# The last level of block inverses in three visits: two pairs of heads one step apart

## The chip, the core and the metric

The kernel runs on one core of a Trainium2 chip. The metric is the time of one execution on the device in microseconds; before the change the median of three runs is 1191.49 (1191.37 to 1192.41).

## The reference, cut to what matters

One layer of a decoder trunk, for 1024 tokens of width 1024 in float32. After an RMSNorm one projection feeds two mixers: four heads of a gated delta rule (head size 128, chunks of 64 in the reference) and eight heads of dilated window attention. Their outputs go through an output projection, a residual, a gated MLP with a causal convolution, and a last norm. The change touches the delta rule, which solves a unit lower triangular system for each chunk and head:

```python
lmat = dec_strict * kk * bc[..., None, :]
rhs = jnp.concatenate([vc, gam * kc], axis=-1)
sol = lax.linalg.triangular_solve(lmat, rhs, left_side=True, lower=True, unit_diagonal=True)
...
def step(state, xs):
    u = uv - jnp.einsum('bhck,bhkv->bhcv', wk, state)
    o = jnp.einsum('bhck,bhkv->bhcv', qd, state) + jnp.einsum('bhcj,bhjv->bhcv', at, u)
    state = ge[..., None, None] * state + jnp.einsum('bhck,bhcv->bhkv', ke, u)
```

## The kernel before

The kernel works with chunks of 128 tokens, so each of the four heads has eight (`NCH`) 128x128 triangles to invert. VectorE inverts the 32x32 blocks on the diagonal (`forward_sub`, line 684). `merges` (line 712) then joins them on TensorE: first 32x32 blocks to 64x64, then, in the part that is changed, 64x64 blocks to 128x128. The transposed result lies in `y` (the tile named um in the profile), one tile for each head; `x64` holds the 64x64 inverses, one tile for a pair of heads (`e` is 0 or 1 within the pair). In that last level every head and chunk needs two products in a row:

- the first ("down") contracts over partitions 0 to 63 (`lo`) and writes a bank's partitions 64 to 127 (`up`), `w2ps`; a copy brings it to `x64[up, e]` (ScalarE for `e` = 0, VectorE for `e` = 1);
- the second ("up") contracts over partitions 64 to 127 and writes partitions 0 to 63, `y2ps`; it reads what the first copy left, and a second copy brings it with its sign turned to `y[lo, :, up]`.

Before, one visit makes the 32 down products of all four heads, a second visit the 32 up products. In the profile a down product is ps<-x,um and an up product ps<-um,x, both 64*64 64x64; each float32 product leaves two matmul records, a product of fp32r operands one. The banks have the tags `asc` and `ch`, two banks each.

The order of instructions on TensorE comes from a planner, the class `Weave` (line 46). Each part of the program is a generator; it yields the time until its operands are ready by the planner's own costs (`need`, line 95, with a slack: `MSLACK` is 1.5 us), and meanwhile the planner runs another part. `mm` (line 191) hands it the cost of a product as its last number, and stamps the products in the order in which they are made. The filler in this stretch is the dense input projection, `dense` (line 508): columns of 128 outputs, each in two halves (`hh`) of eight groups; a group is three products (`mm3`, line 204: xhi,whi, xlo,whi, xhi,wlo, each 128x512). When a half column ends, VectorE scales it out of its bank (`scaled`, line 444, aqkv in the profile); behind the second half come the next weights' split, whi on ScalarE and wlo on VectorE (`split`, line 210), and for some columns a transpose on VectorE (avt).

When all four heads are merged, `chain` (line 811) runs the recurrence over the eight chunks, four heads in turn, with 128x128 products: r,um (the solve), wke,ktok (the new state), ct,kT and ct,qat (with the state ct) and w,qat. Its first products are ps<-vtok,um. The small operations between them (r, wke, ct, vtok) are VectorE's, w is ScalarE's. Attention follows (`attention`, line 915): scores, softmax in tiles sm (a reduction, an exponential on ScalarE, a reciprocal and a multiply on VectorE, two of each a pair of blocks), half transposes of the probabilities (`tp_half`, line 199, ps<-ident,sm) and value products (pt,vn and pb,vc). Then come the output projection and the MLP.

Of the kernel before, what the change touches and what calls it, by code (L numbers as in the profile page):

```python
# [9 lines left out]
AF = mybir.ActivationFunctionType  # L10
OP = mybir.AluOpType
# [7 lines left out]
H = 4  # L19
NCH = 8  # L20
# [16 lines left out]
MSLACK = 1.5  # L37
# [107 lines left out]
def hybrid_layer(tc, I, out):  # L145
    nc = tc.nc
    wv = Weave()
    ve = Engine(wv, nc.vector, "vector", 0.07, 0.00105)
    ac = Engine(wv, nc.scalar, "scalar", 0.12, 0.00085)
# [16 lines left out]
    def tile_(pool, shape, dt, name, tag, bufs):  # L166
        return wv.slot(pool.tile(list(shape), dt, name=name, tag=tag, bufs=bufs), tag, bufs)
# [3 lines left out]
    def A(name, tag, dt=F32, shape=(P, 1024)):  # L171
        if tag in TURNS:
            i = turns[tag] = turns.get(tag, -1) + 1
            tag = TURNS[tag][i % len(TURNS[tag])]
        return tile_(lp, shape, dt, name, tag, SLOTS[tag])
# [12 lines left out]
    def after(inst, anchor, reason="keeps a slot free until it is needed"):  # L188
        tc.add_manual_dep(inst.ins, anchor.ins.name, order, reason=reason)

    def mm(dst, lhs, rhs, us, start=True, stop=True, **kw):
        tc.stamp_issue_order_token(nc.tensor.matmul(dst, lhs, rhs, start=start, stop=stop, **kw).ins, TOKEN)  # L192
        wv.product(us, dst, lhs, rhs)
# [64 lines left out]
    def bank(tag, name="ps"):  # L258
        return tile_(pp_, (P, 512), F32, name, tag, 2)
# [237 lines left out]
    G = [dict() for _ in range(H)]  # L497
# [186 lines left out]
    def forward_sub():  # L684

        mt_t = A("mt", "go")
        sy.dma_start(mt_t, mdram.rearrange("h p f -> (h p) f"))
        mt = mt_t.rearrange("p (j i) -> p j i", j=32)
        xi_t = A("xi", "go")
        xi = xi_t.rearrange("p (i c) -> p i c", i=32)  # L690
        tmp = tile_(sp, [P, 256], F32, "tmp", "t1", 1)
        po_.memset(xi, 0.0)
        po_.affine_select(xi, xi, pattern=[[1, 32], [-1, 32]], compare_op=OP.not_equal, fill=1.0, base=0,
                                channel_multiplier=0)

        free = wv.free["vector"]
        for j in range(31):
            ni, ncol = 31 - j, j + 1
            tv = tmp[:, :ni * ncol].rearrange("p (i c) -> p i c", i=ni)
            ve.tensor_tensor(tv, mt[:, j, j + 1:, None].to_broadcast([P, ni, ncol]),  # L700
                                    xi[:, j, None, :ncol].to_broadcast([P, ni, ncol]), op=OP.mult)
            ve.tensor_tensor(xi[:, j + 1:, :ncol], xi[:, j + 1:, :ncol], tv, op=OP.subtract)

        ve.tensor_copy(mt, xi.rearrange("p i c -> p c i"))
        sy.dma_start(xtdram.rearrange("h p f -> (h p) f"), mt_t)
        anchor = sy.dma_start(xdram.rearrange("h p f -> (h p) f"), xi_t)
        wv.free["vector"] = free
        wv.add(2, merges(anchor))
# [3 lines left out]
    def merges(anchor):  # L712

        tags = ("asc", "ch")
        yield wv.need(xdram)
        ys = [G[h].pop("um") for h in range(H)]
        x64s = []
        for pair in range(2):
            x64 = A("x64", "go", shape=(P, 2, NCH, 64))
            x64s.append(x64)  # L720
            after(po_.memset(x64, 0.0), anchor)
            xd = xdram[2 * pair:2 * pair + 2].rearrange("h (c r) (i j) -> r i (h c) j", r=4, i=32)
            for r in range(4):
                b, o = slice(32 * r, 32 * r + 32), 32 * (r % 2)
                sy.dma_start(x64[b, :, :, o:o + 32].rearrange("p h c j -> p (h c) j"), xd[r])
            for h in (2 * pair, 2 * pair + 1):
                xtd = xtdram[h].rearrange("(c r) (j i) -> r j c i", r=4, j=32)
                for r in range(4):
                    b = slice(32 * r, 32 * r + 32)
                    sy.dma_start(ys[h][b, :, b], xtd[r])  # L730

        heads = [(h, ys[h], x64s[h // 2], h % 2) for h in range(H)]
        halves = [(slice(64 * p, 64 * p + 32), slice(64 * p + 32, 64 * p + 64)) for p in range(2)]

        def four(t):
            return t.rearrange("p (h c j) -> p h c j", h=2, c=NCH)

        w1ps = [bank(t) for t in tags]
        yield wv.need(*w1ps, *x64s, *ys, slack=4.5)
        for h, y, x64, e in heads:  # L740
            for c in range(NCH):
                for a, b in halves:
                    mm(four(w1ps[h // 2])[b, e, c, :], y[a, c, b], x64[a, e, c, 0:32], 0.02)
        w1s = []
        for p in w1ps:
            w1 = tile_(sp, [P, 2, NCH, 32], F32, "w1", "t2", 2)
            w1s.append(w1)
            ac.activation(w1[halves[0][1]], four(p)[halves[0][1]], AF.Copy)
            ve.tensor_copy(w1[halves[1][1]], four(p)[halves[1][1]])
        y1ps = [bank(t) for t in tags]  # L750
        yield wv.need(*y1ps, *w1s, slack=MSLACK)
        for h, y, x64, e in heads:
            w1, y1v = w1s[h // 2], four(y1ps[h // 2])
            for c in range(NCH):
                for a, b in halves:
                    mm(y1v[a, e, c, :], w1[b, e, c, :], y[b, c, b], 0.01)
                b = halves[0][1]
                mm(y1v[b, e, c, :], y[b, c, b], w1[b, e, c, :], 0.02)
        for pair in range(2):
            x64, y1v = x64s[pair], four(y1ps[pair])  # L760
            ve.tensor_scalar(x64[32:64, :, :, 0:32], y1v[32:64], -1.0, None, op0=OP.mult)
            if pair == 1:
                po_.tensor_copy(mark[32:33], x64[32:33, 0, 0, 0:1])
            for i, (a, b) in enumerate(halves):
                for e in range(2):
                    y = ys[2 * pair + e]
                    if (i, e) == (1, 1):
                        ve.tensor_scalar(y[a, :, b], y1v[a, e], -1.0, None, op0=OP.mult)
                    else:
                        ac.activation(y[a, :, b], y1v[a, e], AF.Copy, scale=-1.0)  # L770

        lo, up = slice(0, 64), slice(64, 128)
        w2ps = [bank(t) for t in tags for _ in range(2)]
        yield wv.need(*w2ps, *x64s, *ys, slack=MSLACK)
        w2vs = [p.rearrange("p (c j) -> p c j", c=NCH) for p in w2ps]
        for h, y, x64, e in heads:
            for c in range(NCH):
                mm(w2vs[h][up, c, :], y[lo, c, up], x64[lo, e, c, :], 0.067)
        for h, y, x64, e in heads:
            if e == 0:  # L780
                last["merged"] = ac.activation(x64[up, e], w2vs[h][up], AF.Copy)
            else:
                ve.tensor_copy(x64[up, e], w2vs[h][up])
        wv.done.add("merged")
        y2ps = [bank(t) for t in tags for _ in range(2)]
        yield wv.need(*y2ps, *x64s, slack=MSLACK)
        for h, y, x64, e in heads:
            y2v = y2ps[h].rearrange("p (c j) -> p c j", c=NCH)
            for c in range(NCH):
                mm(y2v[lo, c, :], x64[up, e, c, :], y[up, c, up], 0.067)  # L790
        for h, y, x64, e in heads:
            y2v = y2ps[h].rearrange("p (c j) -> p c j", c=NCH)
            if e == 0:
                ac.activation(y[lo, :, up], y2v[lo], AF.Copy, scale=-1.0)
            else:
                ve.tensor_scalar(y[lo, :, up], y2v[lo], -1.0, None, op0=OP.mult)
            G[h]["yt"] = y
            wv.done.add(("m", h))

    def chain_load(h, s):  # L800
# [285 lines left out]
    last = {}  # L1086
# [696 lines left out]
```

## Time and profile before

| | |
|---|---|
| median of three runs | 1191.49 us |
| profiled execution, time | 1191.63 us |
| its span in the profile | 1189.8 us |
| TensorE busy | 1180.1 us, 99% |
| VectorE busy | 965.4 us, 81% |
| ScalarE busy | 573.2 us, 48% |
| granted TensorE clock, mean | 0.998 |

The page and the answers of the trace name TensorE's matmuls PE, its weight loads PEld, VectorE DVE, ScalarE ACT, GpSimd POOL and the queue that issues most transfers SP. Matmuls are pipelined, so a record is longer than the distance to the next; costs on PE are read from starts. A line of a timeline gives start and length in microseconds, the operation with output<-inputs, its tile sizes and a count of merged records, and in brackets idle time of the engine before it and what ended that.

### The profile page before, as it was taken

The numbers are of one execution on the slowest core, as the hardware profiler recorded it, in microseconds if no ns is written. First come the engines' busy times: TensorE is split into PE (matmuls) and PEld (weight loads), VectorE is DVE, ScalarE is ACT, GpSimd is POOL, SyncE is SP. The second block draws the span as 40 slices with busy tenths as digits, with TensorE's granted clock in tenths as the row PEclk, the third lists the DMA queues.
The fourth block names the chain that finished last, engine by engine and source line by source line (L and its number), as shares of the span: only waits on it lengthen the run. The fifth ranks groups of instructions, "written<-read, shape, count | busy, mean of one in ns | idle before, by whom it ended". The sixth has DMA issues, their size and how long they took to land.

```text
span 1189.8 us, 18253 instructions
## 1 busy us (share of the span) xinstructions
PE 1180.1 (99%) x6994; PEld 975.9 (82%) x6994; DVE 965.4 (81%) x1545; ACT 573.2 (48%) x1122; POOL 54.6 (5%) x49
## 2 busy tenths in 40 slices
PE   9999999999999999999999999999999999999997
PEld 7888888888777777888888888888888888888887
DVE  7776996474677787677998898989889889898987
ACT  7473444363434444555554444545444553546452
POOL 0212001013000000000000000000000000000001
PEclk9999999999999999999999999999999999999999
DMA  7423457647552414343221313122231395356734
GB/s 239 107 94 84 114 144 163 201 149 186 166 147 72 99 37 151 142 159 107 89 92 68 107 53 107 57 103 81 80 102 58 120 377 202 124 178 220 239 98 160
DMA packets 114520, 156.91 MB, mean 132 GB/s; under 512 B 54368, under 2 KB 65408, under 8 KB 114432
## 3 DMA queue, kind: packets, MB, share of 16 engines
q1 hardware_dynamic: 113712, 155.21, 41.4%
q8 instruction: 55, 0.90, 0.3%
q10 hardware_dynamic: 720, 0.53, 0.1%
q14 instruction: 33, 0.27, 0.1%
HBM read 117.68 MB, written 38.03 MB: 131 GB/s over the span
## 4 chain that ended last, share of the span: by engine, by line
PE 97%; DVE 1%; ACT 0%; issue 0%; DVEq 0%; ACTq 0%
PE ps L192 47%; PE pa L192 20%; PE dw L192 18%; PE pc L192 10%; PE ps L201 1%; PE ps L196 1%; PE warm L192 0%; DVE x1h L139 0%; ACT sm L141 0%; DVE sm L141 0%; PE pd L192 0%; DVE avt L139 0%; DVE aqkv L139 0%; DVE wke L141 0%; DVE ct L141 0%
## 5 line engine op out<-in xcount | busy, mean ns | idle before, releaser
L192 PE MATMUL dw<-pr 128*128 128x512 f32 (+1 forms) x984 | 211.4, 376 | 0.0
L192 PEld LDWEIGHTS dw<-pr 128*128 128x128 f32 x984 | 176.7, 188 | 33.7
L192 PE MATMUL ps<-xhi,whi 128*128 128x512 f32 x448 | 183.7, 410 | 0.0
L192 PE MATMUL ps<-xhi,wlo 128*128 128x512 f32 x448 | 175.2, 391 | 0.0
L192 PE MATMUL ps<-xlo,whi 128*128 128x512 f32 x448 | 174.9, 391 | 0.0
L192 PE MATMUL pa<-T,pair 128*128 128x512 f32 x528 | 126.8, 389 | 0.0
L192 PEld LDWEIGHTS pa<-T,pair 128*128 128x128 f32 x528 | 99.1, 188 | 20.6
L192 PEld LDWEIGHTS ps<-xhi,whi 128*128 128x128 f32 x448 | 84.2, 188 | 18.9 <-issue 2.7
L192 PEld LDWEIGHTS ps<-xhi,wlo 128*128 128x128 f32 x448 | 84.1, 188 | 18.3
L192 PEld LDWEIGHTS ps<-xlo,whi 128*128 128x128 f32 x448 | 84.4, 188 | 14.9 <-DVE xlo L139 0.3
L139 ACT ACTIVATE u<-pa 128x512 f32<-128x512 f32 x44 | 26.4, 599 | 114.4 <-PE pa L192 114.4
L139 DVE SCALAR_TENSOR_TENSOR y<-xu,fcw,y 128x1023 f32<-128x1023 f32 (+1 forms) x44 | 56.4, 1281 | 22.1 <-ACT y L139 22.0
L139 ACT ACTIVATE pr<-wd 128x1024 fp32r<-128x1024 f32 x33 | 35.0, 1061 | 73.4 <-DVE wd L139 35.8
L192 PE MATMUL pa<-B,A 128*128 128x512 f32 x264 | 63.5, 389 | 0.0
L192 PE MATMUL pc<-B,pair 128*128 128x512 f32 x264 | 63.4, 389 | 0.0
L192 PE MATMUL pc<-T,S 128*128 128x512 f32 x264 | 63.4, 389 | 0.0
L192 PE MATMUL pa<-T,S 128*128 128x512 f32 x264 | 63.4, 389 | 0.0
L139 DVE TENSOR_TENSOR wst<-wst 128x512 f32<-128x512 f32 x88 | 60.4, 686 | 0.8
L139 ACT ACTIVATE whi<-wst 128x1024 fp32r<-128x1024 f32 (+2 forms) x38 | 38.5, 1013 | 46.5 <-PE ps L192 38.9
L192 PE MATMUL ps<-B,pair 128*128 128x512 f32 x252 | 60.5, 389 | 0.0
L141 ACT ACTIVATE sm<-sm,mx 128x128 f32<-128x128 f32 (+7 forms) x64 | 35.5, 556 | 49.7 <-DVE mx L141 49.7
L192 PEld LDWEIGHTS pa<-T,S 128*128 128x128 f32 x264 | 49.6, 188 | 10.3
(248 smaller groups left out, 2229.8 us busy)
## 6 DMA issues: line engine op xcount, KB each, us to landing
wst<-in_wu SPq DMA_DIRECT2D x44, 512.0 KB, 3.7
wd<-in_wd SPq DMA_DIRECT2D x44, 512.0 KB, 4.4
wst<-in_wi SPq DMA_DIRECT2D x25, 512.0 KB, 4.2
upark<-y SPq DMA_DIRECT2D x22, 512.0 KB, 3.6
r<-upark SPq DMA_DIRECT2D x22, 512.0 KB, 9.9
wa<-in_wd SPq DMA_DIRECT2D x22, 256.0 KB, 3.0
apark<-aqkv SPq DMA_DIRECT2D x8, 512.0 KB, 2.7
wst<-in_wo SPq DMA_DIRECT2D x8, 512.0 KB, 3.6
```

The lines of the kernel that those rows point to most:

```text
L139: return getattr(eng, op)(*a, **kw)
L141: return getattr(eng, op)(*a, **kw)
L192: tc.stamp_issue_order_token(nc.tensor.matmul(dst, lhs, rhs, start=start, stop=stop, **kw).ins, TOKEN)
L196: tc.stamp_issue_order_token(nc.tensor.transpose(dst, src, ident).ins, TOKEN)
L201: tc.stamp_issue_order_token(nc.tensor.transpose(dst, src[rows], ident[rows, rows]).ins, TOKEN)
```

## The change

The last level takes three visits in place of two. The first makes the down products of heads 0 and 1; the second makes the up products of heads 0 and 1 and the down products of heads 2 and 3 in turn, one of each; the third makes the up products of heads 2 and 3. The copies keep their engines. Each visit takes its own banks, and the costs that the planner is told change from 0.067 to 0.06 for a product that stands alone and 0.035 for one in turn. The mark `merged`, for which the values of head 3 wait, is set behind the second visit.

```diff
-        w2ps = [bank(t) for t in tags for _ in range(2)]
-        yield wv.need(*w2ps, *x64s, *ys, slack=MSLACK)
-        w2vs = [p.rearrange("p (c j) -> p c j", c=NCH) for p in w2ps]
-        for h, y, x64, e in heads:
-            for c in range(NCH):
-                mm(w2vs[h][up, c, :], y[lo, c, up], x64[lo, e, c, :], 0.067)
-        for h, y, x64, e in heads:
-            if e == 0:
-                last["merged"] = ac.activation(x64[up, e], w2vs[h][up], AF.Copy)
-            else:
-                ve.tensor_copy(x64[up, e], w2vs[h][up])
-        wv.done.add("merged")
-        y2ps = [bank(t) for t in tags for _ in range(2)]
-        yield wv.need(*y2ps, *x64s, slack=MSLACK)
-        for h, y, x64, e in heads:
-            y2v = y2ps[h].rearrange("p (c j) -> p c j", c=NCH)
-            for c in range(NCH):
-                mm(y2v[lo, c, :], x64[up, e, c, :], y[up, c, up], 0.067)
...
+        w2ps, y2ps = {}, {}
+        for step in range(3):
+            downs = heads[2 * step:2 * step + 2]
+            ups = heads[2 * step - 2:2 * step] if step else []
+            w2ps.update({h: bank(tags[step]) for h, *_ in downs})
+            y2ps.update({h: bank(tags[step % 2 - 1]) for h, *_ in ups})
+            yield wv.need(*[w2ps[h] for h, *_ in downs], *[y2ps[h] for h, *_ in ups], *x64s, *ys, slack=MSLACK)
+            for i in range(2):
+                for c in range(NCH):
+                    for h, y, x64, e in ups[i:i + 1]:
+                        mm(cols(y2ps[h])[lo, c, :], x64[up, e, c, :], y[up, c, up], 0.06 if not downs else 0.035)
+                    for h, y, x64, e in downs[i:i + 1]:
+                        mm(cols(w2ps[h])[up, c, :], y[lo, c, up], x64[lo, e, c, :], 0.06 if not ups else 0.035)
+            for h, y, x64, e in downs:
+                if e == 0:
+                    last["merged"] = ac.activation(x64[up, e], cols(w2ps[h])[up], AF.Copy)
+                else:
+                    ve.tensor_copy(x64[up, e], cols(w2ps[h])[up])
...
+            if step == 1:
+                wv.done.add("merged")
```

The copies of the up products and the marks `("m", h)` that release the chain are as before, at the end of each step and behind the loop.

More of the change, by code (lines that the diff above doesn't have):

```diff
@@ L784, in merges, with cols @@
-        wv.done.add("merged")
-        y2ps = [bank(t) for t in tags for _ in range(2)]
-        yield wv.need(*y2ps, *x64s, slack=MSLACK)
-        for h, y, x64, e in heads:
-            y2v = y2ps[h].rearrange("p (c j) -> p c j", c=NCH)
-            for c in range(NCH):
-                mm(y2v[lo, c, :], x64[up, e, c, :], y[up, c, up], 0.067)
[L791 to L797, printed above, removed]
+        def cols(p):
+            return p.rearrange("p (c j) -> p c j", c=NCH)
@@ new lines, in merges @@
+        w2ps, y2ps = {}, {}
[16 more added lines that the diff above has]
+                    ve.tensor_copy(x64[up, e], cols(w2ps[h])[up])
+            for h, y, x64, e in ups:
+                if e == 0:
+                    ac.activation(y[lo, :, up], cols(y2ps[h])[lo], AF.Copy, scale=-1.0)
+                else:
+                    ve.tensor_scalar(y[lo, :, up], cols(y2ps[h])[lo], -1.0, None, op0=OP.mult)
+                G[h]["yt"] = y
+            if step == 1:
+                wv.done.add("merged")
@@ L798, in merges @@
+        for h in range(H):
             wv.done.add(("m", h))
```

## The prediction

> **What bounds the kernel now.** I read the profile's page first, then who TensorE (PE) waited for, then the busy time by stage, and at the end the timelines of PE and VectorE (DVE) around the changed level and in the stages behind it.
>
> ```profile
> PE 1180.1 (99%) x6994; PEld 975.9 (82%) x6994; DVE 965.4 (81%) x1545; ACT 573.2 (48%) x1122; POOL 54.6 (5%) x49
> PE 97%; DVE 1%; ACT 0%; issue 0%; DVEq 0%; ACTq 0%
> ```
> ```profile
> PE warm L192 <- DVE pick L139: 1.1, 1, 1.1
> PE ps L196 <- DVE rs L139: 0.7, 1, 0.7
> PE ps L192 <- ACT w L141: 0.5, 1, 0.5
> PE ps L192 <- DVE ct L141: 0.4, 1, 0.4
> PE ps L192 <- ACT sq L139: 0.3, 1, 0.3
> PE ps L201 <- DVE sm L141: 0.3, 1, 0.3
> ```
> ```profile
> 560.00:900.00 340.00, 340.00 (x1506) 281.59 (x1505) 302.63 (x345) 164.77 (x217) 0.22 (x1) 1.00 0.25 82
> ```
>
> The first row is the page's busy time, the second its chain that ended last, the six are all of PE's waits (total, times, longest), the last a stage of the MLP. PE carries 97% of the chain, and its waits sum to 3.3 us of 1189.8. In the MLP PE has no gap (340.00 of 340.00 us) with DVE at 302.63. So a microsecond of PE time saved at 210 us comes off the end, unless DVE takes it back before 450 us; behind that each engine's order of instructions is the same in both programs. The change is therefore priced by PE's spacing in its own stretch, and by what DVE does to PE in the two stages after it.
>
> **The two old visits.** In PE's timeline (start, length, operation, count of records) the first visit, the lower-to-upper products of all four heads, stands between dense products:
>
> ```profile
> 209.71 0.39 PE L192 MATMUL ps<-xhi,wlo 128*128 128x512 f32 x1
> 210.02 3.94 PE L192 MATMUL ps<-x,um 64*64 64x64 f32 x64
> 213.90 0.50 PE L192 MATMUL ps<-xhi,whi 128*128 128x512 f32 x1
> 214.23 0.39 PE L192 MATMUL ps<-xlo,whi 128*128 128x512 f32 x1
> 214.46 0.40 PE L192 MATMUL ps<-xhi,wlo 128*128 128x512 f32 x1
> ```
> ```profile
> L192 PE MATMUL ps<-um,x x64: 218/218/267, 218.2 to 221.9; 64*64 64x64 f32 x64
> ```
>
> Dense products start 0.23 us apart (214.23 to 214.46). From 209.71 to 214.46 are 4.75 us; three dense spacings taken off, the visit costs 4.06. A product is two records, so 32 products are 64. The row of the second visit gives their rate: first and last start 3.7 us apart over 63 gaps, 59 ns a record. 64 x 0.059 = 3.78, so about 0.3 us of a visit is change of shape: the entry (0.31 for 0.23), the first gap, and two slow dense starts behind it. The second visit has the same length, so both cost 8.1 us.
>
> **Does taking turns overlap?** All 64 records of an old visit read the same 64 partitions and write the same 64; each starts only when the one before is through. In the middle one of the three new visits a product from the lower to the upper half alternates with one from the upper to the lower, and the two share neither the partitions that they read nor those that they write. The trace has this pattern at two other places, the level of 32x32 blocks (two halves in turn) and the half transposes of attention (two halves of 64 rows in turn):
>
> ```profile
> 196.25 2.21 PE L192 MATMUL ps<-x,um 32*32 32x32 f32 x128
> ```
> ```profile
> 309.48 0.59 PE L201 MATMUL ps<-ident,sm 64*128 64x64 f32 x12
> ```
>
> 2.21 us for 128 records is 17 ns each. The twelve half transposes take 0.59 us from first start to last end, 49 ns each at most, although they too have 64 rows and move 64 columns. Two tiles in turn thus run beside each other, and I take a pair of 64x64 records at the price of one, 59 ns. The bounds: full overlap, or none (59 ns each).
>
> One rule of the Trainium skill speaks against that: "TensorE: Matmul & The Clock Gate", section "Wait — 56ns, not 53.3ns?", says that a sequencer that decodes in microcode spends some 62 ns on each matmul, which then becomes the bound for small ones. By that rule the 59 ns would be an issue rate and turns would gain nothing. The trace doesn't agree, at 17 ns a record. The case stands below as a rival.
>
> **The sum on PE.** The changed kernel's instruction order has three visits: 16 products; 32 in turn; 16, with the first two chain products (vtok) right behind. Each is 32 slots: 32 x 0.059 + 0.3 = 2.2 us, three 6.6. Removed 8.1, added 6.6: **-1.5 us**. Without overlap 128 x 0.059 + 3 x 0.3 = 8.5, +0.4. (The third visit's exit into 128x128 products isn't in the trace; 0 to 0.3 us, and I take it as the same.)
>
> **Copies out of the banks.** ScalarE (ACT) and DVE each copy one head of a pair, as before. Six dense groups (of three products, 0.7 us) stand between the visits, 4.1 us, as long as the plan left before. The last copy is the tight one:
>
> ```profile
> 222.18 0.69 DVE L139 TENSOR_SCALAR um<-ps 64x512 f32<-64x512 f32 x1 [1.18 <-PE ps L192]
> ```
> ```profile
> 223.57 1.05 PE L192 MATMUL ps<-vtok,um 128*128 128x128 f32 x8
> ```
>
> A copy of 64x512 takes DVE 0.69 us and begins 0.1 after the visit. Heads 2 and 3 are wanted by the second two vtok products; two vtok products (four records at 0.11) and one group, 1.1 us, now stand between. Cover 1.1 against 0.8: nothing. Were it gone, 0.8 us at most. No wait is added elsewhere: banks of heads 0 and 1 come free a visit earlier, the loads of the chain keep their place in the SP queue and gain slack, since six more dense groups run before the chain's first use of them.
>
> **What moves.** Those six groups are the second effect. The dense projection is filler whose half columns end every 8 groups with a 128x512 scaling on DVE (aqkv), and every second also with a weight split (whi on ACT, wlo on DVE). Between the first visit and the chain's first state product 20 groups stand now, 14 before; so each end of a half column comes six groups earlier. One such end with a split fell into the densest part of the chain:
>
> ```profile
> 241.19 0.39 PE L192 MATMUL ps<-r,um 128*128 128x128 f32 x2
> 242.03 0.49 PE L192 MATMUL ps<-ct,kT 128*128 128x128 f32 x2 [0.45 <-DVE ct L141]
> ...
> 243.25 0.39 PE L192 MATMUL ps<-wke,ktok 128*128 128x128 f32 x2
> 243.69 0.49 PE L192 MATMUL ps<-ct,qat 128*128 128x128 f32 x2
> ...
> 244.23 0.39 PE L192 MATMUL ps<-r,um 128*128 128x128 f32 x2
> 244.71 0.49 PE L192 MATMUL ps<-ct,kT 128*128 128x128 f32 x2
> ```
> ```profile
> 240.73 1.08 DVE L139 TENSOR_TENSOR aqkv<-ps,rstdB 128x512 f32<-128x512 f32 x1
> 241.64 0.33 DVE L141 SCALAR_TENSOR_TENSOR ct<-ct,ge,ps 128x128 f32<-128x128 f32 x1
> ...
> 242.15 1.22 DVE L139 TENSOR_TENSOR wlo<-wst,whi 128x1024 fp32r<-128x1024 f32 x1
> ```
>
> Two records of a chain product take 0.22 us. From 241.19 to 242.03 PE lost 0.62, from 243.25 to 243.69 0.22, from 244.23 to 244.71 0.26: 1.1 us, behind an aqkv and a wlo that stood before the chain's small operations. In the changed order both come just before and behind the chain's first r, where DVE had room:
>
> ```profile
> 231.93 0.35 DVE L141 SCALAR_TENSOR_TENSOR r<-ps,ngam,vtok 128x128 f32<-128x128 f32 x1 [1.47 <-PE ps L192]
> ```
>
> 1.47 us idle against 1.22 for wlo. So the 1.1 us go. But the next end of a half column, without a split, now falls behind the group at 249.5, between the second of two wke and a state update ct:
>
> ```profile
> 249.90 0.60 DVE L141 TENSOR_SCALAR wke<-ps,ke 128x128 f32<-128x128 f32 x2
> 250.74 0.35 DVE L141 SCALAR_TENSOR_TENSOR ct<-ct,ge,ps 128x128 f32<-128x128 f32 x1 [0.24 <-PE ps L192]
> ```
> ```profile
> 250.09 0.39 PE L192 MATMUL ps<-xhi,wlo 128*128 128x512 f32 x1
> 251.21 0.42 PE L192 MATMUL ps<-ct,kT 128*128 128x128 f32 x2
> ```
>
> That group ends at 250.48; aqkv holds DVE 0.91 us (240.73 to 241.64), so ct starts at 251.4 instead of 250.74, and ct,kT, which followed ct's end by 0.1, comes 0.7 late. Bounds 0 and 1.1. Chain: -1.1 + 0.7 = **-0.4 us** (-1.1 to 0).
>
> **Attention.** One visit of 12 half transposes, that stood alone behind one dense group, now follows the value products directly: one entry and one exit less, 0.1 + 0.1 = **-0.2 us** by the rows at 209.71 and 213.90. The DVE order changes too. One stall came of it before:
>
> ```profile
> 389.10 0.59 PE L201 MATMUL ps<-ident,sm 64*128 64x64 f32 x12
> 390.02 0.60 PE L201 MATMUL ps<-ident,sm 64*128 64x64 f32 x12 [0.33 <-DVE sm L141]
> ```
> ```profile
> 387.21 1.12 DVE L139 TENSOR_TENSOR aqkv<-ps,rstdB 128x512 f32<-128x512 f32 x1
> 388.36 1.25 DVE L139 STREAM_TRANSPOSE avt<-aqkv 128x1024 f32<-128x1024 f32 x1
> ```
>
> The second twelve start 0.92 us after the first; 0.51 would do (a visit of twelve with its exit, 309.48 to 309.99), so 0.4 was lost to aqkv and transpose ahead of the last multiply. 2.4 us of DVE work surfaced as 0.4, so 2.0 were covered. In the new order that transpose, with aqkv and wlo, stands ahead of a whole softmax with one more group to cover it, and in three other softmaxes a lone aqkv stands ahead of the last multiply. 1.1 is under 2.0, also less one group (1.3 left), so they cost nothing by this; bound 0.4 each. I take **-0.2 us** (-0.4 to +1.2).
>
> **Sum.** -1.5 - 0.4 - 0.2 - 0.2 = -2.3 us. The profiled execution took 1191.63 us, 1.8 beside its span of 1189.8, and is 0.14 above the median of 1191.49; nothing of the 1.8 changes. Against the median: 1189.2.
>
> **Rivals.**
> No overlap: the 59 ns are a rate at which records of this size are issued, whatever they read and write. PE then pays +0.4 instead of -1.5, the rest stays -0.8; 1191.1. The 17 and 49 ns rows speak against it: 4%. (By the Trainium skill's rule above it would come out this way.)
> All is covered: aqkv at 250 hides in ct's slack and attention's stall goes: -1.5 - 1.1 - 0.2 - 0.4 = -3.2; 1188.3. For it speaks that the plan places these with DVE's times known to it; against it that it put an aqkv into the chain before and lost 0.6. 21%.
> Slower: DVE becomes the bound behind the change. Nothing of an aqkv inside a softmax or the chain is covered, four at 1.1 us, and the block of aqkv, transpose and wlo (1.1 + 1.25 + 1.2 = 3.6) surfaces but for its one group (0.7): +7.3 against 1.5 + 0.2 + 1.1 + 0.4 = 3.2 gained; 1195.6. It decides from 3.2 us of new waits of PE on DVE upward. The 2.0 us of cover above and DVE's 231.93 gap speak against it: 7%, most of it spread between here and 1192.
> That the turns aren't taken is no case: the built order shows them, record for record.
>
> **The numbers.** My case, 68%, runs from 1188.6 to 1190.2. No change is told from change at about 0.2%, 2.4 us, here 1189.1: right beside the forecast, so a little under half of my case lies beyond it. Faster: 0.68 x 0.4 + 0.21 = 0.48; slower by over 0.2% (above 1193.9): 0.04; within: 0.48. Range 1187.9 to 1191.2: the covered case below, the case without overlap above.
>
> **What would show it.** Right: three visits of 32 slots, about 2.0 us each from first start to last end, the middle one with 64 records at 30 ns; no loss around 241 to 245; a DVE aqkv in the chain some 10 us later, with PE's ct,kT 0.7 behind it. Wrong: a middle visit of 3.9 us, a vtok product that waits for a copy, half transposes that wait for DVE in the second and third pair of attention, or a gap of PE after 450 us.

## The result, and the profile after

The changed kernel takes 1189.77 us (median of 21 runs, 1189.17 to 1190.87), the kernel before, run beside it, 1192.08 (21 runs, 1191.37 to 1193.23). The ratio is 0.9981, 95% interval 0.9975 to 0.9987: 2.3 us faster, where 2.3 had been forecast. (The forecast of 1189.2 stood on a median of 1191.49 from three runs; the 21 runs put the kernel before at 1192.08.) The terms behind the number were not all those of the forecast, as will be seen. The profiled span is 1188.1 us, before 1189.8, both at a mean granted clock of 0.998.

The page's busy times and its chain that ended last, changed kernel:

```profile
PE 1178.3 (99%) x6994; PEld 975.0 (82%) x6994; DVE 964.0 (81%) x1545; ACT 572.8 (48%) x1122; POOL 54.7 (5%) x49
PE 98%; DVE 1%; ACT 0%; issue 0%; DVEq 0%; ACTq 0%
```

All waits of TensorE (total, times, longest, in us):

```profile
PE warm L192 <- DVE pick L139: 1.1, 1, 1.1
PE ps L192 <- DVE ct L141: 0.9, 2, 0.5
PE ps L196 <- DVE rs L139: 0.7, 1, 0.7
PE ps L192 <- ACT w L141: 0.5, 1, 0.5
PE ps L192 <- ACT sq L139: 0.3, 1, 0.3
```

TensorE still carries the chain, and its waits sum to 3.5 us (3.3 before): no row of sm is left, those for ct have grown from 0.4 to 0.9. The three visits in TensorE's timeline:

```profile
210.59 2.07 PE L192 MATMUL ps<-x,um 64*64 64x64 f32 x32
...
216.90 0.27 PE L192 MATMUL ps<-um,x 64*64 64x64 f32 x1
...
217.01 0.22 PE L192 MATMUL ps<-um,x 64*64 64x64 f32 x1
217.02 0.22 PE L192 MATMUL ps<-x,um 64*64 64x64 f32 x1
217.07 0.22 PE L192 MATMUL ps<-um,x 64*64 64x64 f32 x1
217.08 0.22 PE L192 MATMUL ps<-x,um 64*64 64x64 f32 x1
...
218.77 0.22 PE L192 MATMUL ps<-x,um 64*64 64x64 f32 x1
...
223.22 2.08 PE L192 MATMUL ps<-um,x 64*64 64x64 f32 x32
225.23 0.71 PE L192 MATMUL ps<-vtok,um 128*128 128x128 f32 x4
...
226.47 0.61 PE L192 MATMUL ps<-vtok,um 128*128 128x128 f32 x4
```

In the middle visit a um,x and an x,um start 0.01 us apart, and the next such pair 0.06 later (217.01 and 217.02, then 217.07 and 217.08): 64 records start between 216.90 and 218.77, one every 30 ns. So all three visits last as long as 32 records of one kind.

To see where the time went I cut TensorE's trace into stretches. A stretch is what stands between two dense products; it is counted from the start of the last dense product ahead of it to the start of the third one behind it, less three dense spacings of 0.227 us. The table sums them from 205 to 470 us; the part of the third visit that is vtok (0.45 us) is put to the chain:

| us on TensorE | before | changed | difference | forecast |
|---|---|---|---|---|
| visits of the last level | 8.16 | 6.62 | -1.53 | -1.5 |
| chain | 39.59 | 39.93 | +0.34 | -0.4 |
| attention | 68.06 | 67.12 | -0.94 | -0.4 |
| sum | | | -2.13 | -2.3 |

The chain, TensorE and VectorE, around the loss of before at 241 to 245 and around the aqkv that was to come later:

```profile
243.67 0.38 PE L192 MATMUL ps<-wke,ktok 128*128 128x128 f32 x2
243.89 0.39 PE L192 MATMUL ps<-ct,qat 128*128 128x128 f32 x2
```
```profile
252.42 1.05 DVE L139 TENSOR_TENSOR aqkv<-ps,rstdB 128x512 f32<-128x512 f32 x1
253.33 0.31 DVE L141 SCALAR_TENSOR_TENSOR ct<-ct,ge,ps 128x128 f32<-128x128 f32 x1
```
```profile
252.89 0.39 PE L192 MATMUL ps<-r,um 128*128 128x128 f32 x2
253.70 0.49 PE L192 MATMUL ps<-ct,kT 128*128 128x128 f32 x2 [0.42 <-DVE ct L141]
```

The stretch that held the loss now runs at 0.22 us a product (243.67 to 243.89, and so on), and costs 5.57 us for 6.83. Nine microseconds later the aqkv keeps ct back to 253.33, and ct,kT, due at 253.11 (252.89 and 0.22), starts at 253.70: that stretch costs 8.87 us for 8.31. Most of what the chain loses beside that is one more end of a half column, 20 us on, that the prediction had not followed:

```profile
273.09 1.08 DVE L139 TENSOR_TENSOR aqkv<-ps,rstdB 128x512 f32<-128x512 f32 x1 [0.53 <-PE ps L192]
274.01 0.34 DVE L141 SCALAR_TENSOR_TENSOR ct<-ct,ge,ps 128x128 f32<-128x128 f32 x1
```
```profile
273.56 0.39 PE L192 MATMUL ps<-r,um 128*128 128x128 f32 x2
274.40 0.49 PE L192 MATMUL ps<-ct,kT 128*128 128x128 f32 x2 [0.46 <-DVE ct L141]
```

The same picture: an aqkv ahead of a ct, and ct,kT 0.62 late (274.40 for 273.78). This stretch costs 2.29 us for 1.61. Another 0.3 us are lost in a stretch at 284.6, whose cause I did not follow.

### The profile page after: what moved, and what is told of

The parts are those of the page before. It is cut to its first block, busy times and chain, and to the rows that moved or that the text cites. A ratio compares the mean times of both kernels' runs of the same rounds, so it can differ in the third digit from the quotient of the medians.

```text
span 1188.1 us, 18252 instructions
## 1 busy us (share of the span) xinstructions
PE 1178.3 (99%) x6994; PEld 975.0 (82%) x6994; DVE 964.0 (81%) x1545; ACT 572.8 (48%) x1122; POOL 54.7 (5%) x49
## 4 chain that ended last, share of the span: by engine, by line
PE 98%; DVE 1%; ACT 0%; issue 0%; DVEq 0%; ACTq 0%
PE ps L192 47%; PE pa L192 20%; PE dw L192 18%; PE pc L192 10%; PE ps L201 1%; PE ps L196 1%; PE warm L192 0%; DVE x1h L139 0%; ACT sm L141 0%; PE pd L192 0%; DVE aqkv L139 0%; DVE sm L141 0%; DVE wke L141 0%; DVE xr L139 0%; DVE ct L141 0%
## 5 line engine op out<-in xcount | busy, mean ns | idle before, releaser
L192 PEld LDWEIGHTS pc<-T,S 128*128 128x128 f32 x264 | 49.6, 188 | 10.3
```

## The experiments

Three questions: is the gain in the visits the overlap of turns; is the rest the filler's new place; and what makes that place dear or cheap. Times are medians; each ratio is against the runs of the kernel before that were made beside it, whose median was 1191.96 to 1192.49. The stretches of all runs, counted as above, in us:

| kernel | time | ratio | visits | chain | attention |
|---|---|---|---|---|---|
| before | 1192.08 | | 8.16 | 39.59 | 68.06 |
| changed | 1189.77 | 0.9981 | 6.62 | 39.93 | 67.12 |
| e1_blocks | 1190.98 | 0.9990 | 7.96 | 39.95 | 67.10 |
| e2_shift | 1191.43 | 0.9996 | 8.16 | 39.94 | 67.18 |
| e3_cols | 1188.74 | 0.9971 | 4.44 | 39.61 | 68.09 |
| e4_four | 1187.08 | 0.9959 | 3.85 | 39.96 | 67.14 |
| e5_gap9 | 1194.06 | 1.0020 | 3.85 | 42.60 | 70.26 |
| e6_gap5 | 1190.86 | 0.9991 | 3.85 | 43.48 | 68.13 |
| e7_gap10 | 1193.29 | 1.0012 | 3.85 | 42.11 | 71.06 |
| e8_gap5_ot | 1188.69 | 0.9966 | 3.85 | 40.15 | 68.12 |
| e9_gap9_pool | 1193.07 | 1.0003 | 3.85 | 42.15 | 70.22 |
| e10_four_ot | 1187.44 | 0.9957 | 3.85 | 40.94 | 67.11 |

**No turns, same order else.** The middle visit's products in blocks of eight, the up products of one head, then the down products of another:

```diff
                     for h, y, x64, e in ups[i:i + 1]:
                         mm(cols(y2ps[h])[lo, c, :], ...)
+                for c in range(NCH):
                     for h, y, x64, e in downs[i:i + 1]:
```

> The changed kernel, but in its middle visit the 8 up products of a head come in a row, then the 8 down products of the other head, instead of one of each in turn. Every other instruction keeps its place. Theory (turns overlap two tiles): the middle visit takes 64 x 58 ns = 3.7 us from first to last start instead of 1.9, the rest is as in the changed kernel, so the time is 1.9 us over the changed kernel's and about 0.4 under that of before. Rival (the gain is the new placement of the dense groups, not the turns): the time of the changed kernel, 2.3 under before.

1190.98 us, ratio 0.9990 (0.9981 to 0.9999). Chain and attention are those of the changed kernel, the visits 1.34 us dearer: of what turns give, 1.9 expected, blocks keep 0.5. TensorE's timeline at the first border of blocks:

```profile
217.09 0.97 PE L192 MATMUL ps<-um,x 64*64 64x64 f32 x13
217.84 0.27 PE L192 MATMUL ps<-x,um 64*64 64x64 f32 x1
...
217.95 0.22 PE L192 MATMUL ps<-x,um 64*64 64x64 f32 x1
217.95 0.22 PE L192 MATMUL ps<-um,x 64*64 64x64 f32 x1
...
```

Where the block of um,x ends, the first three x,um start beside its last three (the pair at 217.95 is one), ahead of their turn in the program. Three slots of 0.058 us are so saved at each of three borders, 0.52 us. Overlap needs no strict turns, only a product of the other kind within a few records.

One rival is settled by the kernel before. In turns the products also change banks, since each head writes its own; that might be what lets them overlap. In both visits of before, the bank changes from head to head while the partitions stay the same, and there all records but the first start 58 to 59 ns apart, at the changes of bank too. A change of bank alone brings no overlap.

**No turns, filler shifted.** The kernel before, with its second visit later by as much as the changed order has it:

```diff
-        yield wv.need(*y2ps, *x64s, slack=MSLACK)
+        yield wv.need(*y2ps, *x64s, slack=MSLACK + 3.84)
```

> The kernel before with its two visits of 32 products, but the planner waits 3.84 us longer ahead of the second, so that 12 dense groups stand between the two instead of 6. Behind the visits the order on TensorE is then that of the changed kernel, but for one group. Nothing overlaps. Theory: the visits cost 8.1 us as before; what remains is the placement, which in the traces gave -0.7 in the chain's dense part, about +1.0 in its last part and -0.9 in attention: 0.5 to 0.8 us under before. Rival (placement makes the gain): 2.3 under. Rival (placement does nothing): the same as before within 0.2 us.

1191.43 us, ratio 0.9996 (0.9987 to 1.0004). The records of its first visit (minimum, median and longest ns, first and last start):

```profile
L192 PE MATMUL ps<-x,um x64: 218/218/267, 210.2 to 213.9; 64*64 64x64 f32 x64
```

64 records in 3.7 us, as before, and the second visit is like it. But chain and attention are those of the changed kernel within 0.06 us each: +0.35 and -0.88. The interval of the times alone would not tell this from no change; the stretches, each from one profiled execution, do. So the change is two, and they add: the turns -1.5, the new place of the filler -0.5 to -0.6.

**What must differ for an overlap.** The kernel before with its two visits, in which one head of each pair writes the other 64 partitions of its bank; both heads read the same 64. VectorE's copy brings the result to the partitions where it belongs (the up products, not shown, are changed alike):

```diff
-        for h, y, x64, e in heads:
+        for pair in (heads[:2], heads[2:]):
             for c in range(NCH):
-                mm(w2vs[h][up, c, :], y[lo, c, up], x64[lo, e, c, :], 0.067)
+                for h, y, x64, e in pair:
+                    mm(w2vs[h][(up, lo)[e], c, :], y[lo, c, up], x64[lo, e, c, :], 0.035)
...
-                ve.tensor_copy(x64[up, e], w2vs[h][up])
+                ve.tensor_copy(x64[up, e], w2vs[h][lo])
...
```

> The kernel before with two visits, but within each pair of heads the products run in turn and the second head's go to the other half of its bank's partitions; its copy by VectorE moves them back. Two tiles in turn that read the same 64 partitions and write different ones. The dense groups stand as in the kernel before. If it is enough that the written partitions differ: each visit is 32 slots, 32 x 0.058 + 0.3 = 2.2 us instead of 4.1, together 3.7 us under before. If the read partitions have to differ too: no difference from before. A copy that changes partitions might be slower than 0.69 us; nothing on TensorE would show it under 1.1.

1188.74 us, ratio 0.9971 (0.9960 to 0.9982). The records of its first visit:

```profile
L192 PE MATMUL ps<-x,um x64: 218/218/267, 210.5 to 212.4; 64*64 64x64 f32 x64
```

64 records in 1.9 us, and the second visit is like it: other written partitions are enough. Each visit costs 2.22 us, and the two 3.72 less than before; chain and attention stay as before within 0.04, so this is the overlap by itself.

**Both ways at once.** The changed kernel, with e3's edit: two products in turn in the first and third visits, four in the middle one.

```diff
-            for i in range(2):
-                for c in range(NCH):
+            both = ups and downs
+            for c in range(NCH):
+                for i in range(2):
                     for h, y, x64, e in ups[i:i + 1]:
-                        mm(cols(y2ps[h])[lo, c, :], x64[up, e, c, :], y[up, c, up], 0.06 if not downs else 0.035)
-                    for h, y, x64, e in downs[i:i + 1]:
-                        mm(cols(w2ps[h])[up, c, :], y[lo, c, up], x64[lo, e, c, :], 0.06 if not ups else 0.035)
+                        mm(cols(y2ps[h])[(lo, up)[e], c, :], x64[up, e, c, :], y[up, c, up], 0.018 if both else 0.035)
+                    for h, y, x64, e in downs[1 - i:2 - i]:
+                        mm(cols(w2ps[h])[(up, lo)[e], c, :], y[lo, c, up], x64[lo, e, c, :], 0.018 if both else 0.035)
...
```

> The changed kernel's three visits and its order of everything else, with the second head of each pair written to the other half of the partitions: two tiles in turn in the first and third visit, four in the middle one. If it is enough that the written or the read partitions differ: 16 slots a visit, 16 x 0.058 + 0.3 = 1.25 us, three 3.75 instead of 6.6: 2.9 us under the changed kernel, about 5.1 under before. If the read partitions have to differ: the first and the third visit stay, no difference from the changed kernel. If four tiles are too many for the rate of issue, the middle visit stays at 2.2 and the gain is 1.9.

1187.08 us, ratio 0.9959 (0.9946 to 0.9971), the shortest median of all and under both kernels. The middle visit's records:

```profile
L192 PE MATMUL ps<-um,x x32: 218/218/267, 216.3 to 217.3; 64*64 64x64 f32 x32
L192 PE MATMUL ps<-x,um x32: 218/218/267, 216.3 to 217.3; 64*64 64x64 f32 x32
```

64 records start within 1.0 us, some 15 ns each: four run beside each other. Among the four are pairs that read different partitions and write the same ones, so a difference in either is enough. Visits -4.31 us; chain and attention as in the changed kernel.

**Another place for the filler.** If the place counts, a better one may exist. e4 with nine, five and ten dense groups between the visits instead of six, by the planner's slack for the second and third visit:

```diff
-            yield wv.need(..., slack=MSLACK)
+            yield wv.need(..., slack=MSLACK + (1.92 if step else 0))
```

(-0.64 for five groups, 2.56 for ten.)

> The four-tile kernel (two tiles in turn in the first and third visit, four in the second), with 9 dense groups ahead of the second and the third visit instead of 6, by 1.92 us more slack. The ends of the dense half columns then fall outside the chain's densest part: one with a split ahead of the first wke products, one without behind the third w,qat, one with a split behind that part. Theory (the loss comes where DVE's aqkv and wlo meet the dense part of the chain): the visits cost the same 3.75 us, the 0.6 us at the second dense stretch of the chain goes, the last part of the chain and attention change by at most 0.7 either way: 5.1 to 6.2 us under before. Rival (the place of the half columns doesn't matter): as the four-tile kernel, 5.1 under before, with the dense part's stretches unchanged.

> The four-tile kernel with 5 dense groups ahead of the second and the third visit, by 0.64 us less slack. The half columns end behind the first wke products, behind the second ct,kT (with a split) and behind the dense part of the chain: again none in it. The copies still have 3.4 us between visits. Theory: the dense stretches of the chain lose only the 0.8 us that the kernel before lost in its second one without any aqkv: 0.6 less than the four-tile kernel, in all 5.1 to 6.2 under before. Rival (no matter where): 5.1 under, stretches unchanged. If 5 groups don't cover the copies, TensorE waits in the second or third visit.

> The four-tile kernel with 10 dense groups ahead of the second and the third visit, by 2.56 us more slack. An end of a half column with a split (aqkv and wlo on DVE, whi on ScalarE) now falls ahead of the second dense stretch of the chain, where the four-tile kernel has an end without one. Theory: that stretch, 8.86 us of chain products and waits beside three dense spacings there, grows by 0.7 to 1.3, as the first stretch did by 1.26 in the kernel before; 3.8 to 4.6 under before. Rival (no matter where): 5.1 under before, stretch unchanged.

1194.06 us, ratio 1.0020 (1.0010 to 1.0030); 1190.86, 0.9991 (0.9982 to 1.0001); 1193.29, 1.0012 (1.0003 to 1.0021). All three expectations were wrong, though the stretch that I had based them on came out as meant in e5 and e6 (8.31 us each, where e4 has 8.86); in e7 it is 10.9, grown by 2.0 where 0.7 to 1.3 had been expected. What I had bounded at 0.7 us, the later ends of the filler's columns, costs 4.5 to 6.1 us over e4 by chain and attention together. In e5, VectorE, GpSimd and TensorE:

```profile
266.36 1.07 DVE L139 TENSOR_TENSOR aqkv<-ps,rstdB 128x512 f32<-128x512 f32 x1
267.46 1.25 DVE L139 STREAM_TRANSPOSE avt<-aqkv 128x1024 f32<-128x1024 f32 x1
268.63 2.59 DVE L139 TENSOR_TENSOR wlo<-wst,whi 128x1024 fp32r<-128x1024 f32 x1
271.15 0.33 DVE L141 SCALAR_TENSOR_TENSOR ct<-ct,ge,ps 128x128 f32<-128x128 f32 x1
```
```profile
268.25 1.90 POOL L139 TENSOR_TENSOR vtok<-vtok,ms 128x1024 f32<-128x1024 f32 x1
```
```profile
271.54 0.49 PE L192 MATMUL ps<-ct,kT 128*128 128x128 f32 x2 [2.75 <-DVE ct L141]
```

Here is the block of the slower rival: aqkv, avt and wlo, 4.9 us in a row, ahead of a ct for which TensorE waits 2.75 us. And wlo takes 2.59 us in place of 1.22, while GpSimd scales vtok (268.25 to 270.15).

The times of e5 hold something more that its trace does not show. The mean granted clock of its ten executions goes from 0.997 down to 0.994 (e4: 0.997 to 0.998), and the time goes up with it: 1192.80 and 1193.40 at 0.997, 1195.97 and 1195.29 at 0.995, 1195.64 at 0.994. The profiled one is that of 1193.40. Of the 7.0 us between the medians of e5 and e4 its stretches give 5.8; the rest may be the clock, which no trace shows.

In e6, at another place, ScalarE, VectorE and TensorE:

```profile
285.25 0.69 ACT L139 ACTIVATE ot<-ps,gw 128x512 f32<-128x512 f32 x1 [4.51 <-DMA mixer<-ot]
285.83 0.36 ACT L141 ACTIVATE vtok<-ps,rq 128x128 f32<-128x128 f32 x1
```
```profile
286.22 0.35 DVE L141 SCALAR_TENSOR_TENSOR vtok<-ps,gq,vtok 128x128 f32<-128x128 f32 x1 [2.56 <-ACT vtok L141]
```
```profile
286.89 0.49 PE L192 MATMUL ps<-r,um 128*128 128x128 f32 x2 [2.06 <-DVE r L141]
```
```profile
275.14 4.35 SPq L139 DMA_DIRECT2D avdram<-avt  x4
...
280.27 0.69 SPq L139 DMA_DIRECT2D mixer<-ot  x1
```

Read backwards from TensorE: r,um waits for VectorE, VectorE for ScalarE's vtok, which stands behind a copy into ot; and that copy waited 4.51 us for the transfer of an older ot. The last fence is SP's queue: four transfers of avt held it from 275.14 to 279.49, and one of wst came behind them. So the older ot, which ScalarE had begun to write at 275.82, was issued only at 280.27; it had landed by 285.25, when the copy started, at most 5.0 us later.

**Two causes tried.** e8 is e6 with the transfers of ot on ScalarE's own queue; e9 is e5 with most of GpSimd's scaling left out:

```diff
-            sy.dma_start(mixer[h][:, half(hh)], ot)
+            sa.dma_start(mixer[h][:, half(hh)], ot)
```
```diff
-        po_.tensor_tensor(v8(vtok), v8(vtok), ms[:, :, None].to_broadcast([P, NCH, P]), op=OP.mult)
+        wv.account("gpsimd", 0.15 + 0.0021 * 1024, [v8(vtok)], [v8(vtok), ms], 0.28)
+        nc.gpsimd.tensor_tensor(v8(vtok)[:, :, 0:2], v8(vtok)[:, :, 0:2], ...)
```

(The added line tells the planner the old cost, so that the order stays.)

> The kernel of e6 (five groups between the visits, 1190.86 us) with one edit: the transfers mixer<-ot, which carry the delta rule's output away, are issued from ScalarE's queue right behind the copies that write ot, and no longer from SP's. Theory: in e6 TensorE waited 2.06 us at 286.9 for a r of VectorE, VectorE for a vtok of ScalarE, ScalarE stood behind a copy into ot, and that copy for the transfer of an older ot, which SP had issued late, behind the four transfers of avdram (3.72 us on its queue). And the clock of 0.50 from 288 to 291.2 followed from that wait; it cost some 1.6 us more. Then both go: about 3.7 us under e6, 1187.2 us, with a dense spacing of 0.23 us throughout. Rival 1: the wait has another cause (ScalarE's order, the transposes): time as e6, 1190.9, the wait still about 2 us. Rival 2: the wait goes but the clock falls all the same: 1188.8.

> The kernel of e5 (nine groups between the visits, 1194.06 us) in which GpSimd scales 2 of the 128 columns of every chunk of vtok in place of all; the rest of that scaling is left out, all else keeps its order. Theory: in e5 TensorE waited 2.75 us for one ct at 271.5, which stood on VectorE behind aqkv, avt and wlo; wlo took 2.59 us there in place of 1.22 because GpSimd's vtok product ran beside it. Without it wlo takes 1.22 and the wait is 1.4 us: 1.4 under e5, 1192.7 us. Rival: the length of wlo has to do with its own operands or with the transfers beside it: 2.59 and 1194.1 as before.

e8: 1188.69 us, ratio 0.9966 (0.9955 to 0.9978), 3.0 under e6 by the ratios and 3.3 by the stretches, 3.7 expected. The time alone is that of the second rival (1188.8, the clock falls all the same); the trace decides against it. The r,um that stood at 286.89 follows its dense group without a wait, and the clock stays at 1.00. TensorE of e8, then the stage of e6 and of e8 from 288 to 289 us (the column of 0.50 and 1.00 is the granted clock):

```profile
284.88 0.40 PE L192 MATMUL ps<-xhi,wlo 128*128 128x512 f32 x1
285.12 0.38 PE L192 MATMUL ps<-r,um 128*128 128x128 f32 x2
```
```profile
288.00:289.00 1.00, 1.00 (x4) 0.81 (x3) 0.00 (x0) 0.00 (x0) 0.00 (x0) 0.50 0.49 149
```
```profile
288.00:289.00 1.00, 1.00 (x6) 0.81 (x5) 0.30 (x2) 0.40 (x2) 0.15 (x1) 1.00 0.25 59
```

So 3.3 of the 4.5 us that e6 loses to e4 were a late transfer and the low clock that went with it. The clock rests on one profiled execution of each: e6's, at 1192.04 us, is the longest of its ten. The attention of e6 is as dear in e8 (68.13 and 68.12 us, e4 67.14), so this part has another cause.

e9: 1193.07 us, ratio 1.0003 (0.9993 to 1.0012). VectorE's wlo is short again, and the wait for ct half as long:

```profile
269.17 1.18 DVE L139 TENSOR_TENSOR wlo<-wst,whi 128x1024 fp32r<-128x1024 f32 x1
```
```profile
270.67 0.49 PE L192 MATMUL ps<-ct,kT 128*128 128x128 f32 x2 [1.35 <-DVE ct L141]
...
284.64 0.49 PE L192 MATMUL ps<-ct,kT 128*128 128x128 f32 x2 [0.64 <-DVE ct L141]
```

The other 1.35 us are aqkv, avt and wlo themselves. At this place the 1.4 us expected are gained (3.92 us for 5.34), but 0.9 of them are lost again at the ct,kT of 284.64, which did not wait in e5. By the stretches e9 is only 0.5 us under e5. The 2 us by the ratios can't be put down to the scaling alone: the executions of e9 have clocks of 0.996 to 0.998, those of e5 0.994 to 0.997. What e5 and e7 lose in attention against the kernel before (2.2 and 3.0 us; the waits are for sm, pb and pt) I did not follow to its cause.

**Is that transfer a cost in e4 too?** e4 with e8's edit.

> The kernel of e4 (two and four tiles in turn, 1187.08 us) with e8's edit. In e4 ScalarE waited 2.4 us for two transfers of ot, and the chain's last part lost about 1 us at 273 and 285 that the kernel before did not lose. If those losses have e6's cause: 0.5 to 1.0 us under e4, 1186.1 to 1186.6. If those waits of ScalarE are covered by others: 1187.1, no difference. If the issuing on ScalarE (eight transfers) delays the chain's w and vtok: up to 1 us slower than e4, 1188.

1187.44 us, ratio 0.9957 (0.9940 to 0.9974): no difference from e4 that these runs can tell, and an interval that holds all three expectations. The profile speaks against the first: the two stretches that were to get cheaper cost 2.28 and 1.67 us, in e4 2.29 and 1.67. The chain is 1.0 us dearer than e4's, with waits for ScalarE's w of 1.2 us for 0.5, as in the third; but the profiled execution, 1189.28 us, is the longest of four, and the others took 1187.25 to 1187.54. Nothing is gained by it here.

## Why the prediction was right, point by point

- **The overlap** was sized right, and its reason holds: -1.53 for -1.5, 30 ns a record. The 58 ns are the spacing of such records on one part of the array, not a rate of issue: e3 has 30 ns and e4 15 ns a record for products of the same size. Two readings on the way were loose. "Each starts only when the one before is through" is too strong: a record is 218 ns long, and the next starts 59 ns after it. And of the dense starts behind a visit only one is slow (213.90 to 214.23, 0.33 for 0.23), not two; the 0.3 us of a visit stand all the same.
- **The rival without overlap** is out. The Trainium skill's rule for it ("TensorE: Matmul & The Clock Gate", section "Wait — 56ns, not 53.3ns?") gives some 62 ns for each matmul where TensorE decodes in microcode. Turns would have gained nothing by it; the 30 and 15 ns measured here are below it. Whether TensorE decodes so here no run shows.
- **The exit of the third visit**, 0 to 0.3 us, taken as none: 2.65 us with the first vtok products' 0.45, so 2.20 for 2.21 of the first visit. None.
- **The last copy** is covered: the second vtok products start at 226.47, 0.23 behind the dense product ahead of them, without a wait.
- **The loss at 241** is gone: -1.26 for -1.1. **The aqkv at 252** costs +0.55 for +0.7, at the place foretold.
- **The rest of the chain** was the step that failed: taken as unchanged, it costs +1.05 us (0.34 + 1.26 - 0.55), 0.69 of it in one stretch, at 274, by the mechanism that the prediction had just priced at 250. It had followed the ends of half columns to the first two only. So the chain as a whole, +0.34, lies outside its own bounds of -1.1 to 0.
- **Attention** was under-sized: the merged visit is -0.23 for -0.2 (4.32 us for 3.43 and 1.12), but the stalls change by -0.71 more, outside the bounds of the -0.2 that was taken (-0.4 to +1.2). The one shown at 389 is gone, as the covered rival had it:

```profile
390.49 0.96 PE L201 MATMUL ps<-ident,sm 64*128 64x64 f32 x24
```

24 half transposes in one run, a stretch of 1.09 us for 1.65. Other stretches moved by 0.2 to 0.4 either way. One of them is a sign of being wrong that the prediction had named, half transposes that wait for VectorE in the second pair; the lone aqkv ahead of a last multiply, taken as free and bounded at 0.4, costs 0.4 there (1.49 us for 1.09). The wait lies within one row of the timeline, so the list of waits does not have it:

```profile
363.40 1.08 DVE L139 TENSOR_TENSOR aqkv<-ps,rstdB 128x512 f32<-128x512 f32 x1
364.31 0.74 DVE L141 TENSOR_SCALAR sm<-sm,mx 128x384 f32<-128x384 f32 x2
```
```profile
364.14 1.35 PE L201 MATMUL ps<-ident,sm 64*128 64x64 f32 x24
```

- The errors of the two last points, +1.05 and -0.5, cancel in good part: -2.13 by the stretches, where the sum was -2.3. That the sum came nearer than its terms is luck; the visits and the two ends that it followed were right for their reasons.
- **Behind 450 us** nothing is given back: from the output projection to the end the changed trace keeps 1.7 us ahead of the other. (It is not 2.1 mainly because its first visit starts 0.57 us later, 210.59 for 210.02; the profiles of the other runs too differ from that of before, by 0.02 to 1.54 us, ahead of the first visit.)
- **The slower rival** did not decide here, but its mechanism showed in e5, with nine groups between the visits instead of six: the block of VectorE's work, there ahead of a ct. It cost 2.75 us at one place, against the 2.9 (3.6 less 0.7) of the prediction; but half of that came from GpSimd's product beside wlo, which the prediction did not have, so the near match is chance.

## What to carry to other kernels

Small products (64x64 in float32 here) that read or write different partitions ran beside each other when they came in turn: look for a second product, of another head or another step, to put between, and send one of two to the other half of its bank if nothing else differs. Price the shift of the filler as an effect of its own: a control that only shifts (e2) told the two apart, and in the sweep one group less cost 3.8 us and three groups more 7.0 (e6 and e5 beside e4), more than the 1.5 that the overlap of the change brought. Whoever prices a shift must follow every later end of a filler column to the end of the stage, with each engine's queue that it passes, not the first two.

## What the runs showed of the hardware that was not expected

- Products start out of the program's order when they use another part of the array: in e1 three records start early at each border (the x,um of 217.84 is ahead of three um,x that the program has before it).
- VectorE's wlo takes 2.59 us when GpSimd's product on vtok, begun first, runs beside it for 1.52 us (e5), and 1.18 to 1.24 alone. The longer they overlap, the longer it takes: 1.75 us for 0.67 of overlap in the kernel before (at 293.58), 2.44 for 1.36 in e3 (at 290.38). It goes the other way too: where wlo came first, in e8, GpSimd's product took 2.85 us for 1.90:

```profile
290.42 1.24 DVE L139 TENSOR_TENSOR wlo<-wst,whi 128x1024 fp32r<-128x1024 f32 x1
```
```profile
290.56 2.85 POOL L139 TENSOR_TENSOR vtok<-vtok,ms 128x1024 f32<-128x1024 f32 x1
```

The Trainium skill says as much ("SBUF — State Buffer", section "SBUF: two separate sides"): the two engines share a pair of ports that one of them holds for a whole instruction. The traces agree: 1.37 us lost of 1.52 of overlap, and nothing with the scaling left out (e9).
- In the profiled execution of e6 the granted clock was 0.50 from 288 to 291, about 1 us after a wait of 2.06 us, and without the wait it stayed at 1.00 (e8). In that of e5 a wait of 2.75 us was followed by no such fall, though other executions of e5 have a lower mean clock. What makes the difference no run here shows.
